# A hybrid decoder layer on one Trainium2 core: identity added where the state transition leaves PSUM, reciprocal key norms as a power on GpSimd, turned outputs in 96, 96 and 72 rows

## The chip, the core and the metric

The kernel runs on one core of a Trainium2 chip. TensorE (PE) multiplies matrices, VectorE (DVE) and ScalarE (ACT) work elementwise and read PSUM, GpSimd (POOL) works elementwise on SBUF, and SyncE (SP) issues most of the DMAs. Each engine runs its own queue of instructions in order and waits on semaphores for the others. The metric is the device time in microseconds. The kernel before takes 1936.75 us, the median of three runs (1935.41 to 1936.86).

## The reference

One layer of a decoder for 256 new tokens of a prompt and 8 decode tokens, 264 columns in all. A half-step SwiGLU FFN, a mixing stage with two parallel groups of heads, a second FFN, and a final RMSNorm. The mixing stage is sliding-window attention beside RWKV-7 time mixing, of which these lines matter here:

```python
x = x + FFN_RES * swiglu(rmsnorm(x, n1), f1g, f1u, f1d)
...
kk = kk / jnp.maximum(jnp.sqrt(jnp.sum(kk * kk, axis=-1, keepdims=True)), 1e-12)
...
sa = jnp.einsum('bhij,bhj->bhi', S, -kk_t)
S = (S * jnp.exp(lw_t)[:, :, None, :] + sa[..., None] * (kk_t * a_t)[:, :, None, :]
     + v_t[..., None] * k_t[:, :, None, :])
...
y_prompt = rmsnorm(xp, final_norm)
```

## The kernel before

**Layout.** Activations lie with features on partitions: a tile is 128 features by 264 tokens. Weights are streamed from HBM in chunks of 128 x 512 (four blocks of 128 x 128). `chunk` (L129-140) makes of each chunk a rounded part `hi` on ScalarE (L140) and a rest `lo` on VectorE (`tt`, L67), and `gemm` (L143) gives three matmuls of 264 columns for each block (hi·xh, hi·xl, lo·xh; all at L83, the helper `mm`). There are six buffers of raw weights and four each of `hi` and `lo`, so a cast waits until TensorE is through with the chunk four before it. A projection tile of `win` has four chunks, 48 matmuls.

**Stages.** `first_ffn`, then `mixing` (38 projection tiles of `win`, then the output projection `wout` in three passes), then `second_ffn` with the final norm.

**The mixing stage.** The eight pairs of RWKV heads are worked on in four batches of two, as Python generators that `gemm` steps on after each chunk (`tick`); they run beside the projection tiles. `prep` (one for each pair) does the following. It forms the key norms: squares `b`, summed over each head by a matmul with the block of ones `bo` (`nps`, 264 columns), and their reciprocal (`V.reciprocal(b, nps)`, L453). A scan and exponentials make the decays `W`. Then `b` and `kx` are scaled (two scalar-tensor-tensors, an activation with `half` and `less`, a product, and `rk`), which the bonus sum `bps` (`mm(bps, bo, rk)`, 280 columns) and the Gram products of `BK` and `KR` need. `chain` (one for each batch) inverts the triangular part by a substitution on VectorE, forms the transitions `PT` of chunks 1 to 3 and the inputs `N`, and steps the state over them: `Z = wc S + N`, then `S' = wc (PT S) + Z`. In `shifted`, each projection tile is evacuated from PSUM into one of three buffers `pj`; GpSimd copies its last columns to `shc`, and ScalarE and VectorE mix it with the shifted one.

**What sets the order.** The program is written in one order, and a scheduler with a timeline of its own (`schedule_with_timeline_sim=True`) puts each engine's instructions into the order in which they are issued. It decides by its own estimate of when each operand is there; on the chip that order is fixed, whatever the instructions then take.

**The tail.** In `second_ffn`, four of the sixteen output blocks (`ys[2]`) are turned by TensorE into rows of tokens, three pieces of 88 rows, and scaled by `rt`, the reciprocal root of the mean square per token; the other twelve blocks are scaled by a spread of `rt` (`rp`, and `rb` in SBUF) on VectorE and GpSimd and stored by five DMAs on two queues.

Of the kernel before, what the change touches and what calls it, by code (L numbers as in the profile page):

```python
# [42 lines left out]
PX = (1, 2, 1, 1)  # L43
DL = 2
XA = 3
ALPHA = math.exp(-0.5)
LKV = 26
SEQ = [('b', 0), ('b', 1), ('b', 2), ('kv', 0), ('kv', 1), ('kv', 2), ('kv', 3), ('q', 0), ('q', 1), ('q', 2), ('q', 3), ('b', 3), ('q', 4), ('q', 5), ('q', 6), ('q', 7)]
# [7 lines left out]
def body(tc, I, O):  # L56
# [9 lines left out]
    def tt(e, out, a, b, op):  # L66
        return e.tensor_tensor(out=out, in0=a, in1=b, op=op)  # L67

    def stt(out, a, s, b, op0, op1):
        return V.scalar_tensor_tensor(out=out, in0=a, scalar=s, in1=b, op0=op0, op1=op1)  # L70

    def ts(e, out, a, s1, op0, s2=None, op1=None):
        k = {} if op1 is None else dict(op1=op1)
        e.tensor_scalar(out=out, in0=a, scalar1=s1, scalar2=s2, op0=op0, **k)

    def act(out, in_, f, **k):
        return A.activation(out=out, in_=in_, func=f, **k)  # L77

    def bc(ap, shape):
        return ap.broadcast_to(list(shape))  # L80

    def mm(out, lhsT, rhs, start=True, stop=True, **k):
        return TE.matmul(out, lhsT, rhs, start=start, stop=stop, **k)  # L83
# [24 lines left out]
    with ExitStack() as ctx:  # L108
# [259 lines left out]
        def mixing_body(mx, n2, n3, XD, XR):  # L368
# [3 lines left out]
            def ring(shape, tag, bufs):  # L372
                return mx.tile(list(shape), F32, tag=tag, bufs=bufs, name=uid(tag))
# [63 lines left out]
            def prep(p, bt, k, xrr, xk, xv):  # L437
# [12 lines left out]
                yield from pause(PW[0])  # L450
                nps = mp()
                mm(nps[:, :T], bo, b)
                V.reciprocal(b, nps[:, :T])  # L453
# [108 lines left out]
            def chain(bt):  # L562
# [81 lines left out]
                            mm(gb[r, x:x + 64], W[r, k, c - 1, :], bt.Gm[k][h][r, c, 64:128])  # L644
                v = pb[:, :n * 192].rearrange("p (k c t) -> p k c t", k=n, c=3)
                for h in range(2):
                    A.copy(PT[HALF[h]], v[HALF[1 - h]])
# [348 lines left out]
        def second_ffn(n3, xr, XR):  # L996
            fin = Norm(VGF, most=3)

            def load(k):
                if k >= CH:  # L1000
                    n3.split(xr[k], True)

            with tc.tile_pool(name="f2", bufs=1) as fp:
                cur[0] = (fp, NH)
                ys = [fp.tile([P, 4, T], F32, tag="y", bufs=4, name=uid("y")) for _ in range(4)]
                rt = fp.tile([88, 48], F32, name="rt")
                sq = fp.tile([P, NQ, T], F32, name="sq")
                n3.sq = fin.sq = [sq[:, j] for j in range(NQ)]

                def nxt(o):  # L1010
                    fin.square(xr[o])
                    if o == 0:
                        act(rt[:, 7:8], fin.sums[0][0][0:88, 0:1], AF.Sqrt)
                    act(ys[o // 4][:, o % 4], xr[o], AF.Copy, scale=vc(VGF + o))

                def last(ps, x):
                    a, b = slice(0, 176), slice(176, T)
                    q = fin.free.pop(0)
                    u, w = fin.sums[0]
                    tt(G, w, w, u, ALU.add)  # L1020
                    stt(x[:, a], ps[:, a], 0.5, x[:, a], ALU.mult, ALU.add)
                    stt(x[:, b], ps[:, b], 0.5, x[:, b], ALU.mult, ALU.add)
                    tt(V, q[:, b], x[:, b], x[:, b], ALU.mult)
                    act(q[:, a], x[:, a], AF.Square)
                    fin.sums[0] = [w, q]
                    act(ys[3][:, 3], x, AF.Copy, scale=vc(VGF + KD - 1))

                side = dec_state(fp, XR)
                ffn(n3, xr, I["gu2"], I["dn2"], nxt, load, None, side, end=last)
                assert next(side, side) is side  # L1030
                p, ident = fin.sums[0], C[:, CID:CID + P]
                assert len(p) == 2
                sm, rp, again = mp(), mp(), acc()
                turn, keep = [mp(), acc(), mp()], tc.keep_in_program_order
                todo = [(j, o) for j in range(3) for o in range(4)]

                def sums(i):
                    for j in range(3):
                        keep(mm(sm[0:88, j:j + 1], p[i][:, j * 88:j * 88 + 88], ones[:, 0:1], i + j == 0, i == 1, skip_group_check=True))

                def turns(n):
                    for _ in range(n):
                        j, o = todo.pop(0)
                        keep(TE.transpose(turn[j][0:88, o * P:o * P + P], ys[2][:, o, j * 88:j * 88 + 88], ident))

                def spread(to):
                    for j in range(3):
                        keep(TE.transpose(to[:, j * 88:j * 88 + 88], bc(rt[:, j:j + 1], (88, P)), ident[0:88, 0:88]))
# [5 lines left out]
                V.reciprocal(rt[:, 0:3], rt[:, 0:3])  # L1054
                yt = fp.tile([88, 3, 512], F32, name="yt")
# [5 lines left out]
                act(yt[:, 0], turn[0][0:88, :], AF.Copy, scale=rt[:, 0:1])  # L1061
                ts(V, yt[:, 1], turn[1][0:88, :], rt[:, 1:2], ALU.mult)
                SP.dma_start(O["yt"][:, 0], yt[:, 0])
                SP.dma_start(O["yt"][:, 1], yt[:, 1])
                A.copy(rb, again[:, :T])
                act(yt[:, 2], turn[2][0:88, :], AF.Copy, scale=rt[:, 2:3])
                A.dma_start(O["yt"][:, 2], yt[:, 2])
                for e, q, o, n, d, r in ((V, SP, 0, 1, 0, rp[:, :T]), (V, SP, 1, 3, 1, rp[:, :T]), (G, A, 4, 3, 4, rb),
                                         (V, SP, 12, 4, 8, rp[:, :T]), (V, A, 7, 1, 7, rp[:, :T])):
                    y = ys[o // 4][:, o % 4:o % 4 + n]  # L1070
                    tt(e, y, y, bc(r.unsqueeze(1), (P, n, T)), ALU.mult)
                    q.dma_start(O["yT"][:, d:d + n, :], y)

        xsp = [dp.tile([P, T], F32, tag=f"xsp{o}", name=f"xsp{o}") for o in range(KD)]
# [4 lines left out]
        with tc.tile_pool(name="dx", bufs=1) as dx:  # L1079
# [78 lines left out]

def unlay(o):
    y = o["yT"].transpose(2, 1, 0).reshape(T, 12 * P)  # L1160
    y = np.concatenate([y[:, :8 * P], o["yt"].transpose(1, 0, 2).reshape(T, 512), y[:, 8 * P:]], 1)
# [23 lines left out]
```

## Time and profile before

| | before |
|---|---|
| median of three runs | 1936.75 us |
| the profiled execution | 1936.05 us |
| its span, first to last instruction | 1934.2 us |
| granted TensorE clock | 0.999 |
| busy: TensorE, VectorE, ScalarE, GpSimd | 1920.2, 1311.8, 1027.9, 258.2 us |
| HBM read and written | 346.67 and 9.69 MB |
| mixing stage | about 757 to 1149 us |

An instruction's row names line, engine, operation, output<-inputs (without buffer numbers) and shape. Matmuls overlap in the array, so a row's mean duration (284 ns for 264 columns) is longer than the distance of two starts. A busy share says nothing on its own: engines off the path that ends last may idle at no cost. VectorE and ScalarE instructions that follow each other overlap by some tens of ns.

### The profile page before, as it was taken

What the parts mean: (1) busy time and instruction counts of PE and PEld (TensorE: products, weight loads), DVE (VectorE), ACT (ScalarE), POOL (GpSimd) and SP (SyncE); (2) the same over time, 40 slices, a digit from 0 to 9 for tenths busy, and PEclk for the clock granted to TensorE, in tenths of its full rate; (3) what the DMA queues carried; (4) which work ended last, traced back from release to release, by engine and by line L of the source; (5) the groups of instructions that cost most, each with busy time, mean ns of one, the idle gap of its engine ahead of it and who ended that gap; (6) DMA issues with size and microseconds to landing.
All of it is one profiled execution on the core that took longest, in us unless ns stands there. A gap on an engine that the chain in (4) does not pass through costs nothing.

```text
span 1934.2 us, 45549 instructions
## 1 busy us (share of the span) xinstructions
PE 1920.2 (99%) x17171; PEld 1896.7 (98%) x17171; DVE 1311.8 (68%) x2622; ACT 1027.9 (53%) x2041; POOL 258.2 (13%) x376
## 2 busy tenths in 40 slices
PE   9999999999999999999999999999999999999998
PEld 9999999999999999999989999999999999999997
DVE  5865555655556568889888977866666666666655
ACT  5644444444444457676667555644444444444446
POOL 0401101011010113222101100300101001010012
PEclk9999999999999999999999999999999999999999
DMA  7566666665666668655645756666666666666664
GB/s 241 177 192 196 185 195 194 184 191 176 191 183 181 186 183 241 173 165 156 173 124 159 211 155 184 175 188 188 188 195 194 185 193 189 195 195 185 192 181 149
DMA packets 218599, 357.28 MB, mean 185 GB/s; under 512 B 33522, under 2 KB 71938, under 8 KB 218378
## 3 DMA queue, kind: packets, MB, share of 16 engines
q1 hardware_dynamic: 212054, 346.39, 61.0%
q10 hardware_dynamic: 6323, 7.98, 1.3%
q8 instruction: 134, 2.20, 0.5%
q14 instruction: 88, 0.71, 0.1%
HBM read 346.67 MB, written 9.69 MB: 184 GB/s over the span
## 4 chain that ended last, share of the span: by engine, by line
PE 98%; ACT 1%; DVE 0%; DMA 0%; issue 0%; DVEq 0%
PE acc L83 90%; PE m L83 7%; DMA x<-in_x 0%; ACT hi L140 0%; ACT t L77 0%; ACT BT L532 0%; ACT kr L523 0%; PE m L527 0%; PE m L808 0%; PE m L485 0%; DVE y L67 0%; PE m L728 0%; ACT x L953 0%; PE m L809 0%; PE m L810 0%
## 5 line engine op out<-in xcount | busy, mean ns | idle before, releaser
L67 DVE TENSOR_TENSOR lo<-raw,hi 128x512 fp32r<-128x512 f32 (+1 forms) x1288 | 875.3, 683 | 512.2 <-ACT hi L140 490.3
L140 ACT CAST hi<-raw 128x512 fp32r<-128x512 f32 (+1 forms) x1288 | 777.0, 606 | 815.9 <-PE acc L83 742.7
L83 PE MATMUL acc<-x,hi 128*128 128x264 f32 x4840 | 894.5, 286 | 1.0 <-ACT hi L140 1.0
L83 PEld LDWEIGHTS acc<-x,hi 128*128 128x128 f32 x4840 | 750.3, 189 | 6.3 <-issue 2.5
L83 PE MATMUL acc<-x,lo 128*128 128x264 f32 x2420 | 690.8, 286 | 0.2 <-DVE lo L67 0.2
L83 PE MATMUL acc<-h,hi 128*128 128x264 f32 x2752 | 495.0, 284 | 0.0
L83 PEld LDWEIGHTS acc<-x,lo 128*128 128x128 f32 x2420 | 457.2, 189 | 2.2 <-DVE lo L67 0.6
L83 PEld LDWEIGHTS acc<-h,hi 128*128 128x128 f32 x2752 | 424.4, 189 | 0.0
L83 PE MATMUL acc<-h,lo 128*128 128x264 f32 x1376 | 387.8, 284 | 0.0
L83 PEld LDWEIGHTS acc<-h,lo 128*128 128x128 f32 x1376 | 259.2, 189 | 0.0
L67 POOL TENSOR_TENSOR t<-t,t 128x264 f32<-128x264 f32 x74 | 79.9, 1079 | 1096.0 <-DVE t L67 949.8
L83 PE MATMUL acc<-y,hi 128*128 128x264 f32 x648 | 122.7, 284 | 0.0
L83 PE MATMUL acc<-o,hi 128*128 128x264 f32 x648 | 120.1, 284 | 0.0
L83 PE MATMUL acc<-kv,hi 128*128 128x264 f32 x582 | 109.7, 285 | 0.0
L83 PEld LDWEIGHTS acc<-y,hi 128*128 128x128 f32 x648 | 101.2, 189 | 0.1
L83 PEld LDWEIGHTS acc<-o,hi 128*128 128x128 f32 x648 | 100.1, 189 | 0.0
L70 DVE SCALAR_TENSOR_TENSOR x<-acc,x 128x264 f32<-128x264 f32 (+1 forms) x193 | 81.2, 425 | 24.3 <-PE acc L83 23.4
L83 PE MATMUL acc<-y,lo 128*128 128x264 f32 x324 | 92.0, 284 | 0.0
L83 PE MATMUL acc<-o,lo 128*128 128x264 f32 x324 | 92.0, 284 | 0.0
L83 PEld LDWEIGHTS acc<-kv,hi 128*128 128x128 f32 x582 | 89.9, 189 | 0.1
L67 DVE TENSOR_TENSOR t<-acc,t 128x264 f32<-128x264 f32 x156 | 67.4, 432 | 32.8 <-PE acc L83 32.8
L83 PE MATMUL acc<-kv,lo 128*128 128x264 f32 x291 | 82.9, 285 | 0.0
(309 smaller groups left out, 1596.1 us busy)
## 6 DMA issues: line engine op xcount, KB each, us to landing
raw<-in_gu SPq DMA_DIRECT2D x688, 256.0 KB, 3.3
raw<-in_dn SPq DMA_DIRECT2D x224, 256.0 KB, 2.8
raw<-in_win SPq DMA_DIRECT2D x152, 256.0 KB, 3.5
raw<-in_dn SPq DMA_DIRECT2D x160, 192.0 KB, 2.7
raw<-in_wout SPq DMA_DIRECT2D x64, 256.0 KB, 3.5
xsp<-x ACTq DMA_DIRECT2D x16, 132.0 KB, 3.9
x<-xsp SPq DMA_DIRECT2D x16, 132.0 KB, 4.5
ld<-in_sT SPq DMA_DIRECT2D x16, 128.0 KB, 3.1
```

Source lines behind the costliest of these rows:

```text
L67: return e.tensor_tensor(out=out, in0=a, in1=b, op=op)
L70: return V.scalar_tensor_tensor(out=out, in0=a, scalar=s, in1=b, op0=op0, op1=op1)
L83: return TE.matmul(out, lhsT, rhs, start=start, stop=stop, **k)
L140: A.copy(hi[:, :w], raw[:, :w])
```

## The change

Three edits and what goes with them:

1. In `prep`, ScalarE copies the summed squares from PSUM into `b`, and GpSimd raises them to the power -1, taken from a new third column of `eps`, in place of VectorE's reciprocal. This happens eight times.
2. In `chain`, the transition gets the identity where it leaves PSUM: two adds on VectorE for each batch in place of two copies on ScalarE. The step of the state is then one operation, `S' = wc (PT S) + N`, and `Z` is gone.
3. In `second_ffn`, the turned outputs are 96, 96 and 72 rows, `rt` is made by two square roots and two reciprocals, `yt` is stored as 264 rows of 512, GpSimd scales four blocks instead of three, and four stores in place of five go out on exchanged queues.

```diff
+ROWS = ((0, 96), (96, 96), (192, 72))
...
-        eps = cp.tile([P, 2], F32, name="eps")
+        eps = cp.tile([P, 3], F32, name="eps")
+        G.memset(eps[:, 2:3], -1.0)
...
-                V.reciprocal(b, nps[:, :T])
+                A.copy(b, nps[:, :T])
+                tt(G, b, b, bc(eps[:, 2:3], (P, T)), ALU.pow)
...
                 for h in range(2):
-                    A.copy(PT[HALF[h]], v[HALF[1 - h]])
+                    r = HALF[h]
+                    tt(V, PT[r], v[HALF[1 - h]], bc(ident[r, r].unsqueeze(1).unsqueeze(1), (64, n, 3, 64)), ALU.add)
...
-                    Z, Sn = ring((P, n, 64), "Z", 2), ring((P, n, 64), "S", 3)
+                    Sn = ring((P, n, 64), "S", 3)
                     for k in range(n):
-                        stt(Z[:, k], S[:, k], wc[:, bt.p0 + k, c:c + 1], N[:, k, c, :], ALU.mult, ALU.add)
-                    for k in range(n):
-                        stt(Sn[:, k], ps[:, k * 64:k * 64 + 64], wc[:, bt.p0 + k, c:c + 1], Z[:, k], ALU.mult, ALU.add)
+                        stt(Sn[:, k], ps[:, k * 64:k * 64 + 64], wc[:, bt.p0 + k, c:c + 1], N[:, k, c, :], ALU.mult, ALU.add)
...
-                act(rt[:, 0:3], sm[0:88, 0:3], AF.Sqrt, scale=1.0 / D, bias=eps[0:88, 0:1])
-                V.reciprocal(rt[:, 0:3], rt[:, 0:3])
+                for c, n in ((slice(0, 2), ROWS[0][1]), (slice(2, 3), ROWS[2][1])):
+                    act(rt[0:n, c], sm[0:n, c], AF.Sqrt, scale=1.0 / D, bias=eps[0:n, 0:1])
+                    V.reciprocal(rt[0:n, c], rt[0:n, c])
...
-                for e, q, o, n, d, r in ((V, SP, 0, 1, 0, rp[:, :T]), (V, SP, 1, 3, 1, rp[:, :T]), (G, A, 4, 3, 4, rb),
-                                         (V, SP, 12, 4, 8, rp[:, :T]), (V, A, 7, 1, 7, rp[:, :T])):
+                for e, q, o, n, r in ((V, SP, 0, 1, rp[:, :T]), (V, A, 1, 3, rp[:, :T]), (G, SP, 4, 4, rb), (V, A, 12, 4, rp[:, :T])):
...
-OUTS = dict(yT=(P, 12, T), yt=(88, 3, 512), kp=(2, P, P), vp=(2, P, P), ks=(NB, P, 256), vs=(NB, P, 256),
+OUTS = dict(yT=(P, 12, T), yt=(T, 512), kp=(2, P, P), vp=(2, P, P), ks=(NB, P, 256), vs=(NB, P, 256),
```

The first 6,476 large matmuls stand as before on TensorE; from there to the end of the mixing stage the scheduler has set the pieces in between anew. Three places show it. Numbers in names are those of buffers; `acc` rows are large matmuls, line numbers of the change are one to three higher.

First, TensorE at the first pair's bonus sum (`m<-t,C 128x280`). Before:

```order
L83 MATMUL acc_11051<-x_107,lo_11072 128x264
L83 MATMUL acc_11051<-x_108,hi_11089 128x264
L83 MATMUL m_11041<-t_10936,C 128x280
L83 MATMUL acc_11051<-x_108,hi_11089 128x264
L83 MATMUL acc_11051<-x_108,lo_11090 128x264
```

And now:

```order
L84 MATMUL acc_11348<-x_110,hi_11480 128x264 x2
L84 MATMUL acc_11348<-x_110,lo_11481 128x264
L84 MATMUL m_11043<-t_10938,C 128x280
L84 MATMUL m_11154<-tw,ld_11152 128x264
L84 MATMUL m_11156<-la,ld_11152 128x264
L84 MATMUL acc_11503<-x_107,hi_11505 128x264 x2
L84 MATMUL acc_11503<-x_107,lo_11506 128x264
```

The sum stood in the middle of a projection tile, after 6,553 large matmuls; now it stands after 6,720, at the end of a tile, and the next pair's first products (`tw`, `la`) follow it.

Second, VectorE at the scaling of the same pair, from `b` to `rk` (`t_10936`, now `t_10938`). Before:

```order
L453 RECIPROCAL t_10868<-m_10907 128x264
L67 TENSOR_TENSOR pj_10408<-acc_10837,rs 128x264
L67 TENSOR_TENSOR lo_11025<-raw_11023,hi_11024 128x512
L70 SCALAR_TENSOR_TENSOR t_10868<-t_10868,t_10867 128x264
L67 TENSOR_TENSOR lo_11054<-raw_11052,hi_11053 128x512
L70 SCALAR_TENSOR_TENSOR t_10868<-t_10863,t_10868 128x264
L67 TENSOR_TENSOR lo_11072<-raw_11070,hi_11071 128x512
L67 TENSOR_TENSOR bk_10967<-t_10868,t_10911 128x4x2x64
L67 TENSOR_TENSOR t_10863<-t_10863,t_10678 128x264
L67 TENSOR_TENSOR lo_11090<-raw_11088,hi_11089 128x512
L70 SCALAR_TENSOR_TENSOR t_10936<-t_10599,vec,t_10863 128x264
```

And now:

```order
L68 TENSOR_TENSOR lo_11481<-raw_11479,hi_11480 128x512
L68 TENSOR_TENSOR lo_11506<-raw_11504,hi_11505 128x512
L68 TENSOR_TENSOR lo_11601<-raw_11599,hi_11600 128x512
L68 TENSOR_TENSOR lo_11629<-raw_11627,hi_11628 128x512
L68 TENSOR_TENSOR lo_11659<-raw_11657,hi_11658 128x512
L71 SCALAR_TENSOR_TENSOR t_10869<-t_10869,t_10868 128x264
L71 SCALAR_TENSOR_TENSOR t_10869<-t_10864,t_10869 128x264
L68 TENSOR_TENSOR bk_10969<-t_10869,t_10913 128x4x2x64
L68 TENSOR_TENSOR t_10864<-t_10864,t_10679 128x264
L71 SCALAR_TENSOR_TENSOR t_10938<-t_10600,vec,t_10864 128x264
```

The scaling was mixed with the `lo` casts of the running tile; now it stands in one piece, behind the last cast of the tile that ends at the bonus sum (`lo_11481`) and the four casts of the next tile (`lo_11506` to `lo_11659`).

Third, TensorE after the last pair's bonus sum, in the output projection, at the scores (`m<-kv,o`) and the transposes of the probabilities (`m<-C,t`) of two query tiles. Before:

```order
L83 MATMUL m_15716<-kv_110,o_111 128x128
L83 MATMUL m_15715<-kv_110,o_111 128x128
L83 MATMUL acc_15601<-x_109,lo_15766 128x264
L808 MATMUL m_15782<-C,t_15350 128x128
L809 MATMUL m_15782<-C,t_15349 128x128
...
L810 MATMUL m_15788<-C,t_15351 128x128
L83 MATMUL acc_15811<-x_106,hi_15813 128x264 x2
L83 MATMUL acc_15811<-x_106,lo_15814 128x264
```

And now:

```order
L84 MATMUL m_15698<-kv_111,o_112 128x128
L84 MATMUL m_15697<-kv_111,o_112 128x128
L810 MATMUL m_15764<-C,t_15332 128x128
L811 MATMUL m_15764<-C,t_15331 128x128
...
L812 MATMUL m_15770<-C,t_15333 128x128
L84 MATMUL m_15812<-t_15333,kv_111 64x256
L84 MATMUL m_15812<-t_15331,kv_111 64x256
L84 MATMUL m_15845<-kv_111,o_112 128x256
```

Here large matmuls stood between the groups; now scores, transposes and products with the values follow each other directly, and so it goes on for the rest of the attention. In all, TensorE's large matmuls are interrupted 58 times where it was 106.

More of the change, by code (lines that the diff above doesn't have):

```diff
@@ L1005, in second_ffn @@
                 ys = [fp.tile([P, 4, T], F32, tag="y", bufs=4, name=uid("y")) for _ in range(4)]
-                rt = fp.tile([88, 48], F32, name="rt")
+                rt = fp.tile([P, 48], F32, name="rt")
                 sq = fp.tile([P, NQ, T], F32, name="sq")
@@ L1012, in nxt @@
                     if o == 0:
-                        act(rt[:, 7:8], fin.sums[0][0][0:88, 0:1], AF.Sqrt)
+                        act(rt[:, 7:8], fin.sums[0][0][:, 0:1], AF.Sqrt)
                     act(ys[o // 4][:, o % 4], xr[o], AF.Copy, scale=vc(VGF + o))
@@ L1037, in sums, with turns @@
                 def sums(i):
[L1038 to L1042, printed above, removed]
+                    for j, (c, n) in enumerate(ROWS):
+                        keep(mm(sm[0:n, j:j + 1], p[i][:, c:c + n], ones[:, 0:1], i + j == 0, i == 1, skip_group_check=True))
+                def turns(k):
+                    for _ in range(k):
                         j, o = todo.pop(0)
-                        keep(TE.transpose(turn[j][0:88, o * P:o * P + P], ys[2][:, o, j * 88:j * 88 + 88], ident))
+                        c, n = ROWS[j]
+                        keep(TE.transpose(turn[j][0:n, o * P:o * P + P], ys[2][:, o, c:c + n], ident))
                 def spread(to):
-                    for j in range(3):
-                        keep(TE.transpose(to[:, j * 88:j * 88 + 88], bc(rt[:, j:j + 1], (88, P)), ident[0:88, 0:88]))
+                    for j, (c, n) in enumerate(ROWS):
+                        keep(TE.transpose(to[:, c:c + n], bc(rt[0:n, j:j + 1], (n, P)), ident[0:n, 0:n]))
                 sums(0)
@@ L1052, in second_ffn @@
                 sums(1)
-                act(rt[:, 0:3], sm[0:88, 0:3], AF.Sqrt, scale=1.0 / D, bias=eps[0:88, 0:1])
-                V.reciprocal(rt[:, 0:3], rt[:, 0:3])
-                yt = fp.tile([88, 3, 512], F32, name="yt")
+                for c, n in ((slice(0, 2), ROWS[0][1]), (slice(2, 3), ROWS[2][1])):
+                    act(rt[0:n, c], sm[0:n, c], AF.Sqrt, scale=1.0 / D, bias=eps[0:n, 0:1])
+                    V.reciprocal(rt[0:n, c], rt[0:n, c])
+                yt = fp.tile([P, 3, 512], F32, name="yt")
                 rb = tmp()
@@ L1060, in second_ffn @@
                 turns(3)
[L1061 to L1064, printed above, removed]
+                ends = [(rt[0:n, j:j + 1], turn[j][0:n, :], yt[0:n, j], O["yt"][c:c + n]) for j, (c, n) in enumerate(ROWS)]
+                r, x, y, o = ends[0]
+                act(y, x, AF.Copy, scale=r)
+                SP.dma_start(o, y)
+                r, x, y, o = ends[1]
+                ts(V, y, x, r, ALU.mult)
+                SP.dma_start(o, y)
                 A.copy(rb, again[:, :T])
-                act(yt[:, 2], turn[2][0:88, :], AF.Copy, scale=rt[:, 2:3])
-                A.dma_start(O["yt"][:, 2], yt[:, 2])
-                for e, q, o, n, d, r in ((V, SP, 0, 1, 0, rp[:, :T]), (V, SP, 1, 3, 1, rp[:, :T]), (G, A, 4, 3, 4, rb),
-                                         (V, SP, 12, 4, 8, rp[:, :T]), (V, A, 7, 1, 7, rp[:, :T])):
+                r, x, y, o = ends[2]
+                act(y, x, AF.Copy, scale=r)
+                A.dma_start(o, y)
+                for e, q, o, n, r in ((V, SP, 0, 1, rp[:, :T]), (V, A, 1, 3, rp[:, :T]), (G, SP, 4, 4, rb), (V, A, 12, 4, rp[:, :T])):
                     y = ys[o // 4][:, o % 4:o % 4 + n]
                     tt(e, y, y, bc(r.unsqueeze(1), (P, n, T)), ALU.mult)
+                    d = min(o, 8)
                     q.dma_start(O["yT"][:, d:d + n, :], y)
@@ L1160, in unlay @@
     y = o["yT"].transpose(2, 1, 0).reshape(T, 12 * P)
-    y = np.concatenate([y[:, :8 * P], o["yt"].transpose(1, 0, 2).reshape(T, 512), y[:, 8 * P:]], 1)
+    y = np.concatenate([y[:, :8 * P], o["yt"], y[:, 8 * P:]], 1)
     kv = lambda x: np.ascontiguousarray(x.reshape(2, 2, 64, P).transpose(3, 0, 1, 2)).reshape(1, 1, P, 4, 64)
```

## The prediction

> **What bounds the kernel now.** I read the page's head first, then the table by stretches, the waits of TensorE and of the others, and last the timeline around one of the eight reciprocals.
>
> The head:
>
> ```profile
> span 1934.2 us, 45549 instructions
> PE 1920.2 (99%) x17171; PEld 1896.7 (98%) x17171; DVE 1311.8 (68%) x2622; ACT 1027.9 (53%) x2041; POOL 258.2 (13%) x376
> ```
>
> The longest piece of the chain that ended last, the mixing stage in the table by stretches, and four of the eight waits that TensorE has in the whole run (microseconds in total, times, longest), with the largest wait of another engine:
>
> ```profile
> 65.95 691.23 PE acc L83 x5760
> ...
> 757.00:1149.00 392.00, 389.26 (x4442) 367.50 (x4440) 333.74 (x943) 251.29 (x636) 69.57 (x177) 1.00 0.59 167
> ...
> PE m L808 <- DVE kr L67: 0.9, 1, 0.9
> PE m L755 <- issue: 0.7, 1, 0.7
> PE m L83 <- ACT BT L532: 0.5, 1, 0.5
> PE acc L83 <- DVE lo L67: 0.2, 1, 0.2
> ...
> ACT hi L140 <- PE acc L83: 742.7, 992, 3.1
> ```
>
> TensorE is the bound. In the first FFN it issues 5760 large matmuls in 691.23 us, 0.120 us each; the mixing stage (757 to 1149 us, columns PE, PEld, DVE, ACT, POOL) shows it busy 389.26 of 392 us. So hardly anything can be won by a faster VectorE or ScalarE: they wait for TensorE (742.7 us at the `hi` casts alone). What can be lost is much more: any place where TensorE, which runs its queue in order, meets an instruction whose operand is late. Today there is almost no such place.
>
> **The pass on GpSimd.** The eight reciprocals go from VectorE to a copy on ScalarE and a power on GpSimd. The rows nearest to it:
>
> ```profile
> L453 DVE RECIPROCAL t<-m 128x264 f32<-128x264 f32 x8 | 14.4, 1798 | 0.4 <-PE m L83 0.4
> L67 DVE TENSOR_TENSOR t<-t,t 128x264 f32<-128x264 f32 x36 | 16.2, 454 | 0.1
> ...
> L67 POOL TENSOR_TENSOR t<-t,t 128x264 f32<-128x264 f32 x74 | 79.9, 1079 | 1096.0 <-DVE t L67 949.8 <-ACT hi L140 123.4 <-ACT t L77 20.8
> ...
> L262 ACT COPY t<-m 128x264 f32<-128x264 f32 x6 | 2.2, 364 | 0.0
> ```
>
> No row of this trace is a power. Lower bound: one pass of two operands of this shape on GpSimd, 1.08 us. [...] I take 20 steps, 21.6 us, because the same row prices each step, and call it the weakest number here. VectorE is rid of 14.4 us, which it did not owe anybody; ScalarE gets 8 x 0.364 = 2.9 us.
>
> The Trainium skill speaks against this move: GPSIMD Engine Reference, section 4.1, Engine selection, keeps elementwise work on VectorE, at about half the time. The trace agrees, 0.454 against 1.079 us. Section 3.1 of the same page (Elementwise — side-by-side cycle accounting) gives 2.6 cycles an element for two operands and some 12 for a data-dependent branch; at its 1.2 GHz an estimate by that page is 264 x 12 / 1200 = 2.6 us. By it the total would be the first rival's, below.
>
> **The order, which is what matters most.** The scheduler has put TensorE's pieces of the state-space work at other places. Three terms follow.
>
> (a) *Waits at the end of a tile.* In the first place shown above, the bonus sum (`m<-t,C 128x280`) used to stand inside a projection tile; it now stands after the tile's last matmul, and so do those of five other heads. On VectorE the chain which it needs (two scalar-tensor-tensors on `b`, then `kx` and `rk`) now stands behind four `lo` casts of the next tile. These have four buffers, so the fourth cannot be made before TensorE has released the last chunk of the tile that it just finished. TensorE then waits for this sequence, priced from the timeline of VectorE and ScalarE around the first head's present chain:
>
> ```profile
> 790.95 0.42 DVE L70 SCALAR_TENSOR_TENSOR t<-t,t 128x264 f32<-128x264 f32 x1
> 792.78 0.43 DVE L67 TENSOR_TENSOR t<-t,t 128x264 f32<-128x264 f32 x1
> 793.13 0.68 DVE L67 TENSOR_TENSOR lo<-raw,hi 128x512 fp32r<-128x512 f32 x1
> 793.73 0.49 DVE L70 SCALAR_TENSOR_TENSOR t<-t,vec,t 128x264 f32<-128x264 f32 x1
> ...
> 790.92 0.62 ACT L140 CAST hi<-raw 128x512 fp32r<-128x512 f32 x1
> 791.44 0.60 ACT L77 ACTIVATE t<-t,less,half 128x264 f32<-128x264 f32 x1
> ```
>
> 0.62 (hi) + 0.68 (lo) + 0.42 + 0.42 + 0.60 (ScalarE between them) + 0.43 + 0.49 = 3.66 us; hand-overs and GpSimd's 16 columns of `rk` make it 4.2. Six heads: 25 us. At the third of them more VectorE rows stand ahead of the chain; I add 5.
>
> (b) *Runs without a large matmul.* After the last of these six (third place above) the sums, Gram products, transposes, scores and values of two heads and of three query tiles follow each other with no large matmul between, where before some sixteen groups were spread over the output projection. Each needs an evacuation or a softmax of the one before. What that costs when nothing covers it:
>
> ```profile
> 961.00 0.40 DVE t L801
> ...
> 965.91 0.30 PE m L808
> ```
>
> From the first masked maximum to the first transpose lie 4.9 us. Three to four such hand-overs, partly beside each other, are 18 us; a second, shorter run in the third batch (its chain of states and a score tile, eight hand-overs of about a microsecond) is 9. Some twelve single places, where VectorE's bunched chains delay a `lo` cast or a transpose, at about 1.2 us: 15. Sum of (b) 42, between 20 and 55.
>
> (c) *Fewer interruptions.* The large matmuls are interrupted 58 times instead of 106. The cost of one, from TensorE's timeline:
>
> ```profile
> 947.09 0.28 PE L83 MATMUL acc<-x,hi 128*128 128x264 f32 x1
> 947.30 0.69 PE L83 MATMUL m<-TT,W 32*32 32x32 f32 x32
> 947.93 0.40 PE L83 MATMUL acc<-x,hi 128*128 128x264 f32 x1
> 948.16 0.29 PE L83 MATMUL acc<-x,lo 128*128 128x264 f32 x1
> ```
>
> Starts are 0.21 and 0.23 us apart instead of 0.12: 0.20 us for both edges. 48 x 0.20 = 10 us won.
>
> So the order alone gives 25 + 5 + 42 - 10 = +62 us, whatever the power costs, as long as it is covered.
>
> (d) *The power where it is not covered.* Between a head's norm sum (`m<-t,C 128x264`) and its bonus sum now stand 244, 118, 102, 118, 380, 75, 132 and 120 large matmuls. At 0.120 us the first and fifth cover 29 and 46 us, the other six 14.2, 12.2, 14.2, 9 (13 with the small groups there), 15.8 and 14.4: 83.8 us. On each of the six the path is the copy, 0.36, and the pass P; of the wait in (a) the two casts, 1.3, fall away when the power ends last. Excess 6 x (P + 0.36 - 1.3) - 83.8 = 6 P - 89.4 us: nothing below P = 14.9, 40 us at 21.6, 91 at 30. Queued behind the power on GpSimd are the copies into `shc`, which let go of the three `pj` buffers; the next tiles' evacuation waits for them, so a long pass holds TensorE even where the chain would not.
>
> **The identity.** The two copies per batch out of PSUM become adds on VectorE, and the 24 products `Z` go:
>
> ```profile
> L647 ACT COPY PT<-m 64x384 f32<-64x384 f32 x8 | 3.8, 474 | 2.5 <-DVE st L67 1.6 <-PE m L83 0.7
> ...
> L67 DVE TENSOR_TENSOR gm<-m,C 128x512 f32<-128x512 f32 x16 | 10.4, 684 | 0.6 <-PE m L83 0.5
> L67 DVE TENSOR_TENSOR kr<-m,kr 128x192 f32<-128x192 f32 x8 | 2.4, 346 | 0.1
> ...
> L70 DVE SCALAR_TENSOR_TENSOR Z<-S,wc,N 128x64 f32<-128x64 f32 x16 | 3.8, 270 | 0.0
> L70 DVE SCALAR_TENSOR_TENSOR Z<-N,wc 128x64 f32<-128x64 f32 x8 | 1.9, 280 | 0.1
> ```
>
> An add of 384 columns lies between 346 and 684 ns, about 0.56; eight are 4.5 us against 5.7 taken away. `Z` was made beside the products on TensorE and was on nobody's path; 0 us, at worst 8 x 0.1 where the add is late. What hides it is TensorE's own product of the transition with the state (one matmul piece per chunk); in the runs of (b) that cover is thin, but there the chain has become shorter by one product, so I book nothing.
>
> **The tail.** Its present rows:
>
> ```profile
> 1923.77 0.26 ACT L77 ACTIVATE rt<-m,eps 88x3 f32<-88x3 f32 x1 [0.32 <-PE m L83]
> 1924.06 0.17 DVE L1054 RECIPROCAL rt<-rt 88x3 f32<-88x3 f32 x1 [0.94 <-ACT rt L77]
> ...
> 1925.29 1.87 POOL L67 TENSOR_TENSOR y<-y,t 128x792 f32<-128x792 f32 x1 [3.70 <-ACT t L1065]
> ...
> 1927.19 2.01 ACTq L1072 DMA_DIRECT2D out_yT<-y  x2
> ```
>
> Square root and reciprocal come twice: +0.2 us ahead of the scaling. GpSimd gets 1056 columns instead of 792, 1.87 x 4/3 = 2.49, +0.6; VectorE has one 0.42 us product less. The last store leaves at about 1928, as now, with the same bytes in four stores instead of five. +0.3 us, between -0.5 and +1.
>
> **Sum.** 62 + 40 + 0 + 0.3 = +102 us. The profiled execution took 1936.05 us (span 1934.2 and 1.85 around it), 0.7 below the median of 1936.75; 1936.75 + 102 = 2039 us.
>
> **Rivals.** First, *a short power*: P below 14.9 us. For it: other GpSimd passes of this shape take about 1 us (and the skill's page, above). Against it: a power is not one step. Term (d) is nothing, and the time is 1936.75 + 62 = 1999 us, 1979 to 2012 with the bounds of (b).
>
> Second, *a very long power*, P above 30 us: 6 x 35 - 89 = 121 on top of 62, 2120 us and more. Nothing in the trace excludes it.
>
> Third, on the other side, *the waits that I read off the order do not come about*. The mechanism: casts run ahead of TensorE, VectorE has 14.4 + 5.7 us less to do, and the chains of six heads are ready when TensorE gets to the end of the tile. Then only (c) is left, 1936.75 - 10 = 1927 us. It is decided at the last cast before the chain: for it, that cast would have to be possible about 4 us before the tile ends; against it stands the wait of `hi` casts for TensorE, 742.7 us in 992 instances, which says that buffers, not VectorE, hold the casts back.
>
> **Chances.** Forecast (P of 15 to 30) 0.50; short power 0.33; very long power 0.07; the waits that don't come 0.10. About 0.2% (4 us) is what a measurement tells from no change here. Of the last case I give 0.06 to faster, 0.04 to the same; all others are slower, 0.90. The likeliest case alone reaches from 1936.75 + 42 = 1979 to 1936.75 + 75 + 91 = 2103; cut where its ends would need both bounds at once, and with the short power taken in, the range is 1988 to 2095.
>
> **What would show it.** (a): TensorE's waits name VectorE's `t` before the `128x280` sums, 3 to 5 us each at six places. (d): one row for the power on GpSimd; below 15 us the forecast's 40 us fall away and the first rival holds. (b): few large matmuls and most of TensorE's idle time after the last of the eight bonus sums. (c): fewer starts 0.2 us apart. If TensorE's idle time in the mixing stage stays below 10 us, the reading of the order was wrong altogether; if the time is lost in the FFNs or at the end, so was the place.

## The result, and the profile after

The changed kernel takes 2220.42 us (median of six runs, 2218.65 to 2221.22); the kernel before takes 1936.37 beside it (1935.41 to 1938.11). The ratio is 1.1467, interval 1.1455 to 1.1479: slower by 284 us, where the prediction said 102 and ended its range at 2095 us. The sign was right and the size was not.

The head of the profile after, the granted clock in its forty slices, and the engines and lines of the chain that ended last:

```profile
span 2216.6 us, 45554 instructions
PE 1964.1 (89%) x17171; PEld 1928.7 (87%) x17171; DVE 1316.8 (59%) x2598; ACT 1032.1 (47%) x2044; POOL 584.7 (26%) x385
...
PEclk9999999999999986768968775999999999999999
...
PE 79%; POOL 14%; DVE 3%; ACT 1%; DMA 1%; issue 1%; SPq 0%; POOLq 0%; ACTq 0%; DVEq 0%
```

TensorE issues the same 17171 instructions as before, but is busy 1964.1 us instead of 1920.2, and has no work for 252.5 us (span less busy) instead of 14.0. GpSimd, which does not appear in the chain before, is 14% of it. The clock row (`PEclk`, the granted clock in tenths of full speed) says where: full in the first 14 slices and in the last 15, down to 5 to 8 tenths in most of those between.

The first FFN in the chain, in order of time, and the mixing stage in the table by stretches (PE, PEld, DVE, ACT, POOL, then granted clock, DMA share and GB/s):

```profile
65.68 691.23 PE acc L84 x5760
...
757.00:1432.00 675.00, 432.85 (x4440) 399.24 (x4439) 339.37 (x919) 255.67 (x639) 396.06 (x185) 0.79 0.33 97
```

The FFN is as before to the last digit. The mixing stage has grown from 392 to 675 us, and that is the whole loss. VectorE and ScalarE do as much there as before (333.74 and 251.29 us); GpSimd's 69.57 us have become 396.06.

The group that is new on GpSimd, and the waits for it (microseconds in total, times, longest):

```profile
L68 POOL TENSOR_TENSOR t<-t,eps 128x264 f32<-128x264 f32 x8 | 340.1, 42512 | 14.1 <-ACT t L455 10.6 <-ACT ysq L78 3.2
...
ACT t L78 <- DVE t L71: 191.7, 7, 31.4
...
PE m L84 <- POOL t L68: 177.8, 7, 33.7
...
PE acc L84 <- POOL x L68: 27.5, 1, 27.5
```

One power takes 42.5 us. TensorE waits for it seven times, 177.8 us; the same lateness shows as ScalarE's wait for VectorE's scalar-tensor-tensor, which is the chain in between. One more wait, 27.5 us, is for an `x` on GpSimd that is no power. GpSimd's timeline shows why:

```profile
1230.36 42.47 POOL L68 TENSOR_TENSOR t<-t,eps 128x264 f32<-128x264 f32 x1 [4.39 <-ACT t L455]
...
1273.30 1.63 POOL L68 TENSOR_TENSOR x<-y,x 128x264 fp32r<-128x264 f32 x2
```

This `x` is the `lo` half of a `mixed` row, which `split` gives to GpSimd for every other row; two of them took 1.63 us and stood behind a power.

Behind a wait TensorE does not go on at its old speed. Its timeline after the first one:

```profile
832.77 1.29 PE L84 MATMUL m<-t,C 128*128 128x280 f32 x2 [16.15 <-POOL t L68]
...
836.06 0.42 PE L84 MATMUL acc<-x,lo 128*128 128x264 f32 x1
836.28 0.64 PE L84 MATMUL acc<-x,hi 128*128 128x264 f32 x2
836.72 0.42 PE L84 MATMUL acc<-x,lo 128*128 128x264 f32 x1
...
837.23 0.28 PE L84 MATMUL acc<-x,lo 128*128 128x264 f32 x1
837.35 0.41 PE L84 MATMUL acc<-x,hi 128*128 128x264 f32 x2
```

Large matmuls start 0.22 us apart (836.06, 836.28, then two in 0.44 us) until 837, some 4 us after the wait, and 0.12 us apart from then on. The prediction has no term for that.

So the 282.4 us of span are: 177.8 waiting for powers, 27.5 waiting behind one, 33.2 other idle time of TensorE (252.5 less 14.0, 177.8 and 27.5), and 43.9 in which it is busy longer with the same instructions.

### The profile page after: what moved, and what is told of

It is laid out like the page before. It is cut to its first block, busy times and chain, and to the rows that moved or that the text cites. A ratio compares the mean times of both kernels' runs of the same rounds, so it can differ in the third digit from the quotient of the medians.

```text
span 2216.6 us, 45554 instructions
## 1 busy us (share of the span) xinstructions
PE 1964.1 (89%) x17171; PEld 1928.7 (87%) x17171; DVE 1316.8 (59%) x2598; ACT 1032.1 (47%) x2044; POOL 584.7 (26%) x385
## 4 chain that ended last, share of the span: by engine, by line
PE 79%; POOL 14%; DVE 3%; ACT 1%; DMA 1%; issue 1%; SPq 0%; POOLq 0%; ACTq 0%; DVEq 0%
PE acc L84 73%; POOL t L68 14%; PE m L84 6%; DVE st L68 0%; DVE Xt L68 0%; ACT t L78 0%; DVE t L803 0%; DVE t L71 0%; SPq L576 0%; ACT hi L141 0%; DMA Xt<-sa 0%; DVE lo L68 0%; DVE bk L68 0%; DVE t L68 0%; DMA x<-in_x 0%
## 5 line engine op out<-in xcount | busy, mean ns | idle before, releaser
L84 PE MATMUL acc<-x,hi 128*128 128x264 f32 x4840 | 899.2, 288 | 44.3 <-POOL x L68 27.5
L84 PEld LDWEIGHTS acc<-x,hi 128*128 128x128 f32 x4840 | 757.9, 191 | 49.5 <-POOL x L68 27.7
L84 PEld LDWEIGHTS acc<-x,lo 128*128 128x128 f32 x2420 | 461.9, 191 | 2.4 <-DVE lo L68 1.8
L68 POOL TENSOR_TENSOR t<-t,eps 128x264 f32<-128x264 f32 x8 | 340.1, 42512 | 14.1 <-ACT t L455 10.6
L84 PE MATMUL m<-t,C 128*128 128x264 f32 (+1 forms) x32 | 14.2, 532 | 177.8 <-POOL t L68 177.8
L84 PEld LDWEIGHTS m<-t,C 128*128 128x128 f32 x32 | 6.1, 235 | 179.3 <-POOL t L68 179.2
L71 DVE SCALAR_TENSOR_TENSOR t<-t,t 128x264 f32<-128x264 f32 x16 | 8.0, 501 | 174.6 <-POOL t L68 174.3
L78 ACT ACTIVATE t<-t,less,half 128x264 f32<-128x264 f32 x8 | 4.9, 607 | 191.8 <-DVE t L71 191.7
```

## The experiments

Every kernel below is the changed kernel with the edit shown, unless it says otherwise. Ratios are to the kernel before, run on the same chip.

**The reciprocal put back: is the power the whole loss?**

```
-                A.copy(b, nps[:, :T])
-                tt(G, b, b, bc(eps[:, 2:3], (P, T)), ALU.pow)
+                V.reciprocal(b, nps[:, :T])
```

> The reciprocal is back on VectorE, read straight from PSUM; the identity's add and the 96, 96, 72 rows of the tail stay as in the change. Theory (the power is the whole loss): within 0.1% of the kernel before, 1935 to 1938 us, TensorE as good as never without work in the mixing stage (2.7 us before). Rival (the identity's add on VectorE, six passes of a pair, or the new rows cost something that the power hides): 1942 us or more.

1935.26 us beside 1935.55; ratio 1.0000, interval 0.9991 to 1.0009.

```profile
span 1934.9 us, 45520 instructions
PE 1921.5 (99%) x17171; PEld 1899.3 (98%) x17171; DVE 1311.8 (68%) x2606; ACT 1024.2 (53%) x2034; POOL 258.4 (13%) x377
```

The identity's add and the 96, 96, 72 rows neither gain nor lose: TensorE is without work for 13.4 us, as before.

**The power alone**, put into the kernel before (the diff's lines at the norms and at `eps`, nothing else).

> The kernel before with the power alone: ScalarE's copy out of PSUM and the power on GpSimd. Theory (the power is the whole loss): 2215 to 2225 us, as the whole change. Rival (the edits act together, the identity's later VectorE work adding to the waits): under 2205 us.

2215.99 us, ratio 1.1450 (1.1433 to 1.1468). Its power takes the same time:

```profile
L67 POOL TENSOR_TENSOR t<-t,eps 128x264 f32<-128x264 f32 x8 | 340.1, 42512 | 14.1 <-ACT t L454 10.8 <-ACT ysq L77 3.1
```

The two runs settle which part of the change it is. What remains is how 42.5 us, eight times, become 284.

**A short pass in the power's place.** The way through the engines stays: ScalarE's copy, a pass on GpSimd, then VectorE.

```
-                tt(G, b, b, bc(eps[:, 2:3], (P, T)), ALU.pow)
+                tt(G, b, b, bc(ones[:, 0:1], (P, T)), ALU.mult)
+                V.reciprocal(b, b)
```

> The change with its way through the engines kept (ScalarE's copy out of PSUM, a pass of 264 columns on GpSimd), but with GpSimd's pass a product with ones, about 1.1 us, in place of the power; VectorE's reciprocal follows, so what is computed is the same. Theory (the way costs nothing while the pass is short, only the power's length does): within 0.2% of the kernel before, 1933 to 1941 us. Rival (to leave VectorE for ScalarE and GpSimd and come back costs by itself, each chain being some 3 us longer, eight chains): 1945 us or more.

1938.57 us beside 1935.61; ratio 1.0013, interval 1.0004 to 1.0022, +3 us. The pass took 0.64 us, not the 1.1 expected. Here the scheduler leaves the bonus sums within 32 large matmuls of where they stood before. So the detour by itself costs about 3 us for eight heads, in an order close to the old one; the rest comes with the power's length, through the waits and through the order that the scheduler makes for it. The order does go by that length: between the first head's norm sum and its bonus sum stand 92 large matmuls here, 160, 198 and 244 with the power on 66, 96 and 132 columns below, and 244 in the change. The first rival's case, a short power in the changed order, was therefore not run, and its 62 us are not tested here.

**The power on fewer columns.** VectorE's reciprocal does the rest, so what is computed stays the same and only the power's length changes. With 132 columns the power takes what the prediction had taken; with 96 it ends about where the prediction let its cover end. With 198 the edit reads

```
-                A.copy(b, nps[:, :T])
-                tt(G, b, b, bc(eps[:, 2:3], (P, T)), ALU.pow)
+                A.copy(b[:, :198], nps[:, :198])
+                V.reciprocal(b[:, 198:], nps[:, 198:T])
+                tt(G, b[:, :198], b[:, :198], bc(eps[:, 2:3], (P, 198)), ALU.pow)
```

and the others have 132, 96 and 66 in the place of 198.

> As the run with 132 columns, the power on 66 columns alone, VectorE's reciprocal on the other 198; some 10.6 us for a power, and an order of TensorE between that of before and that of the change (71 runs of large matmuls broken off in place of 101 and 53). Theory 1 (the order costs up to 62 us by itself, as the prediction had it): 1960 to 1999 us. Theory 2 (there is no cost of the order; a power under about 11 us lies behind large matmuls): within 8 us of the kernel before. Rival (in proportion to the power): +71, 2007 us.

> The power on 96 columns, VectorE's reciprocal on the other 168; 15.5 us for a power, just where the prediction let the cover end, in an order that has five of the eight bonus sums behind the same matmuls as the change. Theory 1 (the prediction's order, +62, and almost no wait for the power): 2001 us. Theory 2 (interpolated between the runs with 66 and 132 columns): 2005 us, with under 50 us in which TensorE has no work. Rival (the order is free, the loss begins with the first power that is not covered): under 1980 us.

> The change with the power on columns 0 to 131 alone; VectorE's reciprocal does the other 132 straight from PSUM, so what is computed is the same. At the 161 ns per column that the whole power showed it should take 21.3 us, the 21.6 that the prediction had taken, and the order of TensorE's matmuls stays nearly that of the change. Theory 1 (the prediction's sum holds, only the price of the power was wrong): 62 + 6 x 21.3 - 89 = +100, 2037 us. Theory 2 (the sum itself is short, since the slower matmuls behind each wait are not in it): 2050 to 2075 us, with TensorE busy 15 to 30 us longer than before. Rival (the loss is in proportion to the power): 284 x 21.3 / 42.5 = +142, 2079 us.

> The power on 198 columns, VectorE's reciprocal on the other 66; 31.9 us for a power. Theory 1 (six waits that grow with the power, the prediction's slope): 62 + 6 x 31.9 - 89 = +164, 2100 us. Theory 2 (about eight us for each us of a power, the slope between 132 and 264 columns: more than six waits, and the slower clock behind them): +112 + 8.1 x 10.6 = +198, 2134 us.

Of each kernel, in that order, the engines' row, then the power's group (with 66 and 198 columns one power takes 11.04 and 32.00 us), and the waits that count (the wait for `x` is 1.4 us with 96 columns and 16.9 us with 198):

```profile
span 1966.1 us, 45564 instructions
PE 1937.3 (99%) x17171; PEld 1907.3 (97%) x17171; DVE 1314.6 (67%) x2606; ACT 1025.9 (52%) x2042; POOL 343.3 (17%) x385
...
PE m L84 <- POOL t L68: 1.5, 2, 1.1
```

```profile
span 2009.0 us, 45551 instructions
PE 1951.4 (97%) x17171; PEld 1920.3 (96%) x17171; DVE 1319.2 (66%) x2606; ACT 1027.4 (51%) x2042; POOL 374.9 (19%) x385
...
L68 POOL TENSOR_TENSOR t<-t,eps 128x96 f32<-128x96 f32 x8 | 125.3, 15663 | 9.5 <-ACT t L455 9.5
...
PE m L84 <- POOL t L68: 18.7, 4, 7.7
PE acc L84 <- ACT hi L141: 10.0, 4, 8.0
```

```profile
span 2043.3 us, 45557 instructions
PE 1952.5 (96%) x17171; PEld 1919.7 (94%) x17171; DVE 1320.7 (65%) x2606; ACT 1030.6 (50%) x2044; POOL 418.7 (20%) x385
...
L68 POOL TENSOR_TENSOR t<-t,eps 128x132 f32<-128x132 f32 x8 | 171.5, 21444 | 10.5 <-ACT t L455 7.9 <-ACT ysq L78 2.6
...
PE m L84 <- POOL t L68: 46.8, 4, 15.3
PE acc L84 <- POOL x L68: 7.1, 1, 7.1
```

```profile
span 2128.4 us, 45560 instructions
PE 1962.2 (92%) x17171; PEld 1926.1 (90%) x17171; DVE 1319.4 (62%) x2606; ACT 1031.8 (48%) x2044; POOL 502.1 (24%) x385
...
PE m L84 <- POOL t L68: 108.9, 6, 23.7
```

Worked out from these rows against the span of before, 1934.2 us, with 1920.2 busy (the prediction's sum is 62 + 6P - 89.4, and 62 at most below P = 14.9):

| columns | power, us | time, us | ratio | over before | prediction's sum | waits for power and `x` | other idle time | longer busy |
|---|---|---|---|---|---|---|---|---|
| 66 | 11.0 | 1969.43 | 1.0176 (1.0162 to 1.0190) | 34 | up to 62 | 1.5 | 13.3 | 17.1 |
| 96 | 15.7 | 2008.60 | 1.0376 (1.0361 to 1.0392) | 73 | 67 | 20.1 | 23.5 | 31.2 |
| 132 | 21.4 | 2047.47 | 1.0574 (1.0560 to 1.0589) | 112 | 101 | 53.9 | 22.9 | 32.3 |
| 198 | 32.0 | 2130.16 (one run) | | 194 | 165 | 125.8 | 26.4 | 42.0 |
| 264 | 42.5 | 2220.42 | 1.1467 (1.1455 to 1.1479) | 284 | 228 | 205.3 | 33.2 | 43.9 |

Three things follow. Given the right P, the prediction's sum is 6 and 11 us short at 15.7 and 21.4 us, and 29 and 56 us short at 32.0 and 42.5. The loss is not in proportion to the power (the rivals of 2007 us with 66 columns and 2079 us with 132 are out by 38 and 32). And with 66 columns, where TensorE waits 1.5 us for a power, 34 us are lost all the same, half of them while it is busy: theory 2 of that run, no cost of the order, falls, and theory 1 holds.

The other expectations came out in part. With 96 columns both theories' times are near (2001 and 2005 us), but TensorE is without work for 57.6 us where theory 2 had under 50; the rival falls. With 132 columns the time lies between theory 1 (2037 us) and the range of theory 2 (2050 to 2075), and TensorE is busy 32.3 us longer where theory 2 had 15 to 30. With 198 columns theory 2 (2134 us) is near and theory 1 (2100) is 30 us short.

**Where the busy time comes from.** With 66 columns the granted clock tells. First TensorE alone just before the stretch at the end of the mixing stage and its wait there, then the stretch itself with all engines, and last the same 40 us of the run in the kernel with the reciprocal back:

```profile
1095.74:1099.15 3.41, 2.80 (x90) 1.00 0.62 148
...
1101.41 1.22 PE L84 MATMUL m<-kv,o 64*128 64x256 f32 x4 [2.57 <-ACT kr L547]
...
1100.00:1132.00 32.00, 27.06 (x222) 20.22 (x222) 24.93 (x125) 17.55 (x70) 4.65 (x12) 0.50 0.25 70
```

```profile
1100.00:1140.00 40.00, 40.00 (x549) 38.52 (x548) 30.12 (x71) 17.61 (x33) 1.21 (x1) 1.00 0.52 148
```

In a run of sums, scores and values without large matmuls the granted clock falls to 0.50 at 1099.15 us and stays there for 34 us, until large matmuls have come back. TensorE's wait of 2.6 us for ScalarE is not what lowered it: that wait lasts from 1098.84 to 1101.41 us, so the clock fell 0.3 us after it began. In the 3.41 us before, TensorE was busy for 2.80 us at full clock, but with small matmuls alone (most of them 64x2 and 64x64). The kernel with the reciprocal back shows the same once, at 940.39 us: 3.41 us without a large matmul, 2.63 of them busy, and then one step of 3.41 us at 0.50. So runs of small matmuls can lower the clock without a long wait.

What a wait does was measured by itself: the kernel with the reciprocal on VectorE, and behind its last output a row of tests, in which nothing else runs.

```
+                def row(k):
+                    for _ in range(k):
+                        keep(mm(pa[:, :T], wr, xm))
+
+                def wait(k):
+                    act(seed[:, 0:k], pa[:, 0:k], AF.Identity, scale=0.0, bias=ones[:, 0:1])
+                    tt(G, seed[:, 0:k], seed[:, 0:k], bc(eps[:, 2:3], (P, k)), ALU.pow)
+                    keep(mm(pa[0:k, 0:64], seed[:, 0:k], ones[:, 0:64]))
+
+                row(100)
+                for k in (2, 8, 16, 24, 32, 48):
+                    wait(k)
+                    row(100)
+                wait(16)
+                for _ in range(300):
+                    keep(mm(pa[0:64, 0:64], ones[0:64, 0:64], ones[0:64, 0:64]))
+                row(100)
```

> The change with the reciprocal on VectorE, and behind the last outputs a row of tests: 100 large matmuls, then a wait for ScalarE and a power of 2, 8, 16, 24, 32 and 48 columns, each followed by 100 large matmuls that need nothing; at last a wait of 16 columns, 300 matmuls of 64x64 and 100 large ones. Theory (a wait lowers TensorE's clock): behind the longer waits, from some 3 us on, large matmuls start 0.22 to 0.24 us apart and after about 4 us 0.11 to 0.12 us apart; behind the shortest they start 0.11 us apart at once; the 64x64 ones don't bring the full clock back. Rival (the slower large matmuls behind the waits of the change come from late weights or other queues): 0.11 us apart behind every wait.

TensorE's timeline (start, duration of a group, the idle time before it in brackets; each of the small f32 matmuls stands as two records), and some of the same stretches with PE's busy time, then granted clock, DMA share and GB/s:

```profile
1943.63 0.27 PE L84 MATMUL acc<-ones,seed 128*2 128x64 f32 x2 [1.22 <-POOL seed L68]
1943.84 12.27 PE L84 MATMUL acc<-xm,wr 128*128 128x264 f32 x100
1958.24 0.28 PE L84 MATMUL acc<-ones,seed 128*8 128x64 f32 x2 [2.14 <-POOL seed L68]
1958.45 13.84 PE L84 MATMUL acc<-xm,wr 128*128 128x264 f32 x100
...
2039.30 0.45 PE L84 MATMUL acc<-ones,seed 128*48 128x64 f32 x2 [8.53 <-POOL seed L68]
2039.67 14.77 PE L84 MATMUL acc<-xm,wr 128*128 128x264 f32 x100
2057.84 0.28 PE L84 MATMUL acc<-ones,seed 128*16 128x64 f32 x2 [3.40 <-POOL seed L68]
2058.06 63.64 PE L84 MATMUL acc<-ones 64*64 64x64 f32 x600
```

```profile
1958.00:1972.00 14.00, 13.76 (x101) 0.88 0.01 1
...
2075.00:2121.00 46.00, 46.00 (x434) 0.50 0.01 1
```

A wait of 1.22 us costs nothing beside itself: 100 large matmuls take 12.27 us at full clock. Behind 2.14 us they take 13.84, behind 8.53 us 14.77, and behind the lengths between 13.93 to 15.07. So a long wait costs about 2.5 us on top of itself when large matmuls follow it. When 64x64 matmuls follow, the clock sinks to half and stays there for the 63.64 us that they last, with TensorE busy all that time. That the granted clock and not late weights makes these matmuls slow is shown: in these stretches the DMAs bring 1 GB/s, and the matmuls are slow where the clock is 0.50. The threshold was set too high: some 3 us were expected, and 2.14 was enough. Behind 2.14 us and the first 3.40 us the clock falls 1.6 and 1.2 us after the wait has ended, and it comes back 3.41 us later. Each length but 3.40 us was tried once.

The Trainium skill has a rule for it: TensorE: Matmul & The Clock Gate, Part 1, says that an idle window of about 3.4 us, in a free-running count, halves TensorE's clock and that a busy one of about the same length restores it. The trace agrees on the halving and, for large matmuls, on the recovery (4 us behind the first wait of the changed kernel); it differs for small ones, which kept TensorE busy for 46 us at 0.50, and for the idle time that is enough: 2.14 us in the test, and no more than 0.6 of 3.41 us ahead of the fall at 1099.15.

**GpSimd's queue.** The `lo` halves of `split` are all given to VectorE, so that none stands behind a power.

```
-                tt((G, V)[i % 2], lo[:, :n], mixed[i][:, :n], hi[:, :n].bitcast(F32), ALU.subtract)
+                tt(V, lo[:, :n], mixed[i][:, :n], hi[:, :n].bitcast(F32), ALU.subtract)
```

> The change with the four `lo` halves of `mixed` that GpSimd subtracts before the last pass moved to VectorE, so that no split stands behind a power in GpSimd's queue. Theory (the wait of 27.5 us for `x` on GpSimd adds to the others): 2185 to 2200 us. Rival (the next power is late anyway, so the wait goes over to the next bonus sums): 2212 us or more.

2215.70 us, ratio 1.1448 (1.1429 to 1.1467): 5 us of the 27.5, if any. The time is the rival's. The two waits that stand there now:

```profile
1275.25 1.30 PE L84 MATMUL m<-t,C 128*128 128x280 f32 x2 [8.50 <-POOL t L68]
1329.93 1.29 PE L84 MATMUL m<-t,C 128*128 128x280 f32 x2 [43.71 <-POOL t L68]
```

8.5 and 43.7 us, 52.2 together, for 27.5 and 31.5 (59.0) in the changed kernel. But this edit moved more than a queue. In its order 294 large matmuls stand between the seventh head's norm sum and bonus sum (132 in the changed kernel), and none between the last head's (120 there). For these covers terms (a) and (d) of the prediction give 10.5 and 45.8 us, so the two waits are about what the powers' own lateness makes of the new order. What GpSimd's queue costs by itself this run can't say, and the rival's mechanism, a wait that passes on, is not shown by it.

## Why the prediction was wrong

**Term (d), the price of the power.** This is the step that failed. It took 20 steps of 1.079 us, 21.6 us, and let P reach 30 in the forecast; the row says 42.5, twice the one and well over the other. No run shows a power as a number of such steps: the 20 was a guess, multiplied by a row of another operation, and the 30 was no bound. The 2.6 us that the prediction worked out from the Trainium skill (GPSIMD Engine Reference, section 3.1) are a sixteenth of what the row says. In the prediction's own sum the difference is 6 x (42.5 - 21.6) = 125 us, the larger part of the 182 that were missing. The second rival, a very long power, is the case that came, at 0.07; its 2120 us and more had P = 35. By its own arithmetic 42.5 us give 6 x 42.5 - 89.4 + 62 = +228, 2165 us. (One small slip has no weight: with (b) at 20 the order costs 25 + 5 + 20 - 10 = 40 us and not 42, so the lower end of 1979 us should be 1977.)

**Terms (a) and (d) for one head were right.** For a head with 118 large matmuls as cover they say 4.2 + P + 0.36 - 1.3 - 14.2 = P - 10.9: 31.6 us at 42.5, 21.1 at 32.0 and 10.5 at 21.4. TensorE's timelines of the changed kernel, of 198 and of 132 columns have

```profile
885.72 1.29 PE L84 MATMUL m<-t,C 128*128 128x280 f32 x2 [31.27 <-POOL t L68]
```

```profile
865.76 1.29 PE L84 MATMUL m<-t,C 128*128 128x280 f32 x2 [20.71 <-POOL t L68]
```

```profile
924.37 1.29 PE L84 MATMUL m<-t,C 128*128 128x280 f32 x2 [10.18 <-POOL t L68]
```

within 0.4 us. The places were right as well: each is a bonus sum that the scheduler had put behind its tile's last matmul. They name GpSimd's `t` and not VectorE's, since the power ends last; the three to five microseconds that (a) expected of VectorE alone were not seen by themselves. With 66 columns three bonus sums still stand behind their tile's last matmul, and TensorE waits 1.1 us at one of them and not at all at the two others. Even where the power is about covered, at 96 columns, the waits name GpSimd (18.7 us) and a `hi` cast (10.0).

**The count of waits drifted.** The formula holds six heads. At 42.5 us the first head's 244 matmuls, 29 us, no longer cover it either (16.15 us at 832.77), the fifth head waits 1.9 us, and TensorE's wait for `x` stands where the seventh's would. By the formula (a) and (d) are 30 + 165.6 = 196; the waits for powers and for `x` are 205.3. Worked out in the same way for all eight heads (16.5 us for the first and 0.2 for the fifth, and without the 5 us that (a) adds at one head) it is 208. The prediction named GpSimd's queue as a danger, but for the copies into `shc`; what TensorE waited for was the split of `mixed`. For the seventh head the formula has 30.0 us where TensorE waits 27.5 for `x`, so nothing shows that this queue cost anything beside the power's own lateness; no run takes the two apart.

**Terms (b) and (c).** Term (b) is idle time, 42 us, between 20 and 55. The idle time beside the waits for the power is 33.2 us, within these bounds, but not at the place that was named: from 1335 us, after the last bonus sum, TensorE is idle for 9.7 of the next 47 us (37.31 busy), and the rest lies scattered. Term (c), 10 us won, would show as less busy time, and TensorE is busy longer; the sum by the clock below leaves less than 1 us for it.

**What was missing: the clock.** 43.9 us of the loss are slower matmuls, and no term stood for them. Some of it can be placed by an estimate from the test of single waits: six of the waits for the power are of 16 us and more, and one is for `x`; seven times 2.5 us are 18. The run of small matmuls at the end adds about as much. Its stretch in the changed kernel:

```profile
1335.00:1382.00 47.00, 37.31 (x365) 28.18 (x366) 30.82 (x151) 26.05 (x101) 4.56 (x12) 0.57 0.25 73
```

37.31 us busy at a clock of 0.57, which would be some 21 at the full one: 16 us. Together 34 of 43.9. The trace gives the rest too. In the changed kernel's mixing stage the granted clock is 0.50 in 14 stretches, from 819.96 to 1383.16 us; added up, with TensorE's busy time in them:

```profile
sum 286.72, PE 89.32; mean PE 6.38
```

At full clock 89.32 us would be half, so by this estimate the low clock costs 44.7 us, all of the 43.9. The same sum gives 15.9, 33.1, 31.8 and 40.3 us for 66, 96, 132 and 198 columns, where TensorE is busy 17.1, 31.2, 32.3 and 42.0 us longer. In the kernel before the clock is 1.00 throughout that stage.

This also corrects what the table seems to say for the sum at 96 and 132 columns. There it came within 6 and 11 us because two errors met: with 132 columns the added idle time is 76.8 us where the formula has 111 (its 101 and the 10 of (c)): 53.9 for 69 in (a) and (d), since four heads and `x` waited and not six heads, and 22.9 for 42 in (b). The clock's 32.3 us filled the gap. The +62 for the order alone was not measured as such: no kernel had the changed order with a short pass, since the scheduler makes the order from the pass's length. At 66 and 96 columns, on either side of where the cover should end, 34 and 73 us were lost, but in orders that are not quite the change's, and 17.1 and 31.2 us of it are slower matmuls. The added idle time is 14.8 and 43.6 us, where (a) and (b) have 72. So the size of 62 may be near, but not what it was added up from.

**The identity and the tail** were priced at 0 and +0.3, and the kernel with both and without the power is the same as before within 0.1%.

## What to carry to other kernels

Rows of other operations give no upper bound for an operation that no row shows; if the whole forecast hangs on its length, say what the time is at two and four times the guess and keep that in the range. When the bound is TensorE, price a wait for it twice: the wait itself, and the slower matmuls behind it, about 2.5 us where large ones follow and as long as the run lasts where only small ones do. Price long runs of small matmuls without a wait, too: they can lower the clock by themselves. A pass moved to an idle engine is free only if it is shorter than the work that stands between its operand and its reader, so count that work first. Even then it may cost something through the order: with 66 columns the power was covered but for 1.5 us, and 34 us were lost.

## What the hardware showed that I had not expected

A power of GpSimd takes 0.16 us for each column of 128 rows, whatever the length: 15.66, 21.44 and 42.51 us for 96, 132 and 264 columns, and in the test of waits

```profile
1942.85 0.73 POOL L68 TENSOR_TENSOR seed<-seed,eps 128x2 f32<-128x2 f32 x1 [15.79 <-ACT seed L78]
...
2031.24 8.00 POOL L68 TENSOR_TENSOR seed<-seed,eps 128x48 f32<-128x48 f32 x1 [15.46 <-ACT seed L78]
```

(8.00 - 0.73) / 46 = 0.158 us a column and 0.41 us to begin with, against 0.64 us for 264 columns of a product with a broadcast column. VectorE's reciprocal of the same tile is 1.80 us, 24 times less than the power.

A wait of 2.14 us was enough to slow TensorE afterwards, 1.22 us was not; and 64x64 matmuls, issued without a gap, held it at half clock for as long as they lasted. Small matmuls also took it there without a long wait (at 1099.15 us with 66 columns, at 940.39 us with the reciprocal back). In the mixing stage of these traces the granted clock changes only in whole steps of 3.41 us: in the changed kernel at 819.96, 837.03 and 857.51 us, 5 and 6 steps apart, and so on. So where a wait lies against these steps may count as well as its length; that was not tested.
